# Latent attention of a two-layer encoder, written out as a fixed order of blocks on one Trainium2 core

## The chip, the cores and the metric

The kernel runs on one core of one Trainium2 chip. The metric is the device time of one execution in microseconds (us). Five engines work side by side, each through its own list of instructions: TensorE (PE in the profile, its weight loads PEld), VectorE (DVE), ScalarE (ACT), GpSimd (POOL) and SyncE (SP), which here only issues DMAs.

## The reference, cut to what matters

A trunk of two layers over 512 tokens of width 1024. Layer 0 is neighbourhood attention and a dense SwiGLU, layer 1 latent attention and a top-2-of-8 expert SwiGLU. The latent attention is what the change touches:

```python
c_q = _rmsnorm(down[..., :256]) * q_norm
c_kv = _rmsnorm(down[..., 256:384]) * kv_norm
q = (c_q @ w_uq).reshape(B, S, 16, 64 + 32)
kv = (c_kv @ w_ukv).reshape(B, S, 16, 64 + 64)
k_nope, v = kv[..., :64], kv[..., 64:]
...
s = (q_nope . k_nope + q_rope . k_rope) * scale      # 16 heads, 512 x 512
p = softmax(s, axis=-1)
o = p @ v                                            # then o @ w_o
```

Each of the two layers also has six vectors of 1024 values, `c_act @ w_ada[i] + b_ada[i]`, which shift, scale and gate its two halves.

## The kernel before, in words

All products that need full precision are made of three TensorE passes over a rounded part ("hi", `...H`) and a rest ("lo", `...L`). A split is therefore a cast of a tensor on ACT and a subtraction on DVE or POOL. `split_piece` is one such pair; `passes` (lines 295 to 297) issues the three matmuls.

The weights come through a list of jobs (`plan`). A job loads a raw tile (three slots), splits it (three slots) and is emitted when `need` first asks for it or looks ahead to it. Jobs of the kind "ada" add w_ada rows, weighted by c_act, into an accumulator on DVE (lines 223 and 225, eight per vector). The list strews the vectors (0, 2) to (1, 4) between the jobs of the first layer; vector (1, 5) stands behind the latent attention's weights (`add_ada(1, 5)`), and so falls in that stage.

`mla_phase` does the latent attention. Its loop goes over 8 pairs of heads; in a pair first the one head, then the other, each in four blocks of 128 queries against all 512 keys. A block is: three score matmuls of 512 columns; the row minimum of the (negated) scores on DVE (line 951); the exponential with its row sum on ACT (line 954); reciprocal and multiplication on DVE (955, 956); four transposes on TensorE (959); a copy out of PSUM on ACT (960). After a head's blocks `project(h + 2)` makes the queries of a later head (six matmuls; multiplication with the rotary table on DVE, cast on ACT, subtraction on POOL) and for every second head the keys of a pair (three matmuls, two splits). After both heads the products with the values follow (line 966): eight of 512 columns, then a split into `oH`, `oL`. Weights that fall due (`uq` 1, `mla_o`) are split by `need`, every second piece of 1024 columns on POOL (`MLA_POOL`).

None of this has an order of its own: a scheduler chooses before the run which instruction follows which on each engine, and it also places matmuls of the next stage (`mm<-oH`, `mm<-oL`: the output projection, three at a time in `mm` tiles of PSUM) into the attention. Two other parts of the kernel, the start (line 566) and the experts (line 1413), stand under `tc.manual_schedule()`: there each engine runs the block's instructions in the order in which the code issues them. Instructions from outside the block can still be placed between them.

PSUM is full: three `mm` tiles, two for scores, two for transposes, one for the sums `po`.

Of the kernel before, what the change touches and what calls it, by code (L numbers as in the profile page):

```python
# [19 lines left out]
P = 128  # L20
S = 512
D = 1024
KD = D // P
NH = 16
HD = 64
# [20 lines left out]
NKT = 3  # L46
MLA_POOL = 2
NQB = 4
# [10 lines left out]
class Kernel:  # L59
# [35 lines left out]

    def add_ada(self, layer, which):
        for j in range(4):
            self.jobs.append(("ada", (layer, which, j)))
# [336 lines left out]
    def plan(self):  # L435

        d = self.d
# [11 lines left out]
        bg = [(0, 2), (0, 3), (0, 4), (0, 5)] + [(1, w) for w in range(5)]  # L449
        bg = [(l, w, j) for l, w in bg for j in range(4)]  # L450
# [32 lines left out]
        self.add_ada(1, 5)  # L483
# [343 lines left out]
    def mla_phase(self, xT, hH, hL, norm):  # L827
        nc, tc, d = self.nc, self.tc, self.d
        scale = 96.0 ** -0.5
        with ExitStack() as es:  # L830
            pool = lambda name, bufs, **kw: es.enter_context(tc.tile_pool(name=name, bufs=bufs, **kw))
            st = self.mlap = pool("mla_static", 1)
            w2 = pool("mla_w2", 2)
            w3 = pool("mla_w3", 3)
# [13 lines left out]
            sq = w2.tile([P, 4, S], F32, name="pT")  # L848
            sq = [sq[:, i] for i in range(2)]
# [60 lines left out]
            qk = {}  # L910

            def project(h):
                hi, lo = self.need(("uq", h // 8), 0 if h < 2 else 1 if h < 8 else 2)
                ps = self.proj(hi, lo, h % 8, [cq[0][:, k] for k in range(2)], [cq[1][:, k] for k in range(2)], 2)
                q = [queries[:, h % NQB * 2 + z] for z in range(2)]
                t = self.stat2.tile([P, S], F32, name="t", tag="tmp")
                nc.vector.tensor_mul(t, ps, rope)
                nc.scalar.copy(q[0], t)
                (nc.gpsimd if h > 1 else nc.vector).tensor_tensor(q[1], t, q[0].bitcast(F32), op=OP.subtract)
                qk[h] = (q, kt[h % NKT])  # L920
                if h % 2:
                    return
                ps = self.mm.tile([P, S], F32, name="mm", tag="mm")
                wh, wl = (w[:, h:h + 2].rearrange("p h c -> p (h c)") for w in self.wk)
                self.passes(ps, wh, wl, ckv[0][:, 0], ckv[1][:, 0], True, True)
# [4 lines left out]
            queries = self.new_big("queries", F32R)  # L930
            oH, oL = self.new_big("oH", F32R), self.new_big("oL", F32R)
            self.pool_every = MLA_POOL
            with tc.high_priority():
                project(0)
                for k in kt[1:]:
                    for z in range(2):
                        nc.scalar.copy(k[z][64:128], kt[0][z][64:128].bitcast(F32))
                project(1)
            for pair in range(NH // 2):
                po = ps_o.tile([P, S], F32, name="po")  # L940
                PT = []
                for hh in range(2):
                    h = 2 * pair + hh
                    q, k = qk.pop(h)
                    pT = w2.tile([P, 4, S], F32, name="pT")
                    PT.append(pT)
                    for b in range(4):
                        s = ps_s.tile([P, S], F32, name="s")
                        self.passes(s, *(z[:, b * P:(b + 1) * P] for z in q), *k, True, True)
                        nm = w3.tile([P, 1], F32, name="nm")  # L950
                        nc.vector.tensor_reduce(nm, s, axis=AX.X, op=OP.min)
                        e = w3.tile([P, S], F32, name="e")
                        den = w3.tile([P, 1], F32, name="den")
                        nc.scalar.activation(e, s, AF.Exp, bias=nm, scale=-1.0, accum_out=den)
                        nc.vector.reciprocal(den, den)
                        nc.vector.tensor_scalar_mul(e, e, den)
                        pt = ps_t.tile([P, 4, P], F32, name="pt")
                        for t in range(4):
                            nc.tensor.transpose(pt[:, t], e[:, t * P:(t + 1) * P], self.ident)
                        nc.scalar.copy(pT[:, :, b * P:(b + 1) * P], pt)  # L960
                    if h + 2 < NH:
                        project(h + 2)
                for t in range(4):
                    for hh in range(2):
                        h = 2 * pair + hh
                        nc.tensor.matmul(po[hh * 64:hh * 64 + 64], V[:, t, h * HD:(h + 1) * HD], PT[hh][:, t],
                                         start=t == 0, stop=t == 3)
                self.split_piece(oH[:, pair], oL[:, pair], po)
            self.pool_every = 0
# [761 lines left out]
```

## Time and profile before

| | us |
|---|---|
| median of 3 runs | 1646.46 (1645.37 to 1647.16) |
| profiled execution | 1649.19 |
| its span, first to last instruction | 1647.3 |

The profile comes from that one profiled execution. Its times count from the first instruction of the span. A busy engine in a stretch is the sum of its instructions' times, and a matmul's time overlaps the next one's; so the distance between two starts is what a matmul takes of TensorE, not its duration. "[0.55 <-ACT hH]" behind an instruction means that its engine stood idle for 0.55 us before it, and that ACT's work on hH ended the wait.

### The profile page before, as it was taken

To read this page: it belongs to the slowest core of one execution; us is meant where nothing else is said; L and a number is where in the kernel's file an instruction comes from. 1 tells how busy PE (TensorE), PEld (TensorE's weight loads), DVE (VectorE), ACT (ScalarE), POOL (GpSimd) and SP (SyncE) were. 2 spreads that over 40 slices of the span, in tenths; PEclk is the share of its full clock that TensorE was granted. 3 is DMA by queue.
4 is the path that set the end of the run, shared out by engine and by line. 5 is a ranking of instruction groups with operands and counts; after the bars stand their busy time and mean duration, and the time that the engine had idled before them with its cause. 6 is when DMAs were issued, how large, how long until landed. Compare 5 with 4: busy or idle time off the path is not lost. (4 is left out here: it accounts for less than half of the span.)

```text
span 1647.3 us, 23092 instructions
## 1 busy us (share of the span) xinstructions
PE 1572.5 (95%) x7909; PEld 1245.2 (76%) x7909; DVE 1107.1 (67%) x1688; ACT 819.9 (50%) x1384; POOL 310.9 (19%) x259
## 2 busy tenths in 40 slices
PE   6899999999999999989999989999999999999996
PEld 4677779888888888856668677778887777777885
DVE  4687855765655434698865668656447888887765
ACT  3455544422222123577663656545436677765442
POOL 0332310002000000021101343112123324233310
PEclk9999999999999999999999989999999999999998
DMA  9545533467544523222112599758568999997751
GB/s 355 186 141 166 169 119 103 146 216 253 194 160 158 193 77 112 74 77 77 52 65 69 182 360 355 256 187 259 175 192 295 334 351 357 345 371 260 262 192 53
DMA packets 241209, 327.38 MB, mean 199 GB/s; under 512 B 9586, under 2 KB 191570, under 8 KB 240404
## 3 DMA queue, kind: packets, MB, share of 16 engines
q1 hardware_dynamic: 231072, 296.19, 54.0%
q0 software_dynamic: 5232, 18.09, 3.0%
q10 hardware_dynamic: 4740, 11.02, 1.8%
q8 instruction: 89, 1.46, 0.4%
q14 instruction: 76, 0.62, 0.1%
HBM read 308.75 MB, written 16.52 MB: 197 GB/s over the span
## 5 line engine op out<-in xcount | busy, mean ns | idle before, releaser
L198 DVE TENSOR_TENSOR lo<-raw,hi 128x1024 fp32r<-128x1024 f32 (+1 forms) x284 | 374.9, 1350 | 92.4 <-ACT hi L195 84.8
L195 ACT CAST hi<-raw 128x1024 fp32r<-128x1024 f32 (+1 forms) x319 | 318.3, 1045 | 225.0 <-PE mm L296 146.3
L296 PE MATMUL mm<-hL,hi 128*128 128x512 f32 x480 | 190.7, 397 | 0.0
L295 PE MATMUL mm<-hH,hi 128*128 128x512 f32 x480 | 190.1, 396 | 0.1
L297 PE MATMUL mm<-hH,lo 128*128 128x512 f32 x480 | 190.1, 396 | 0.0
L1245 PE MATMUL gu<-hi,he 128*128 128x512 f32 x360 | 144.5, 401 | 9.6 <-ACT act L1255 3.9
L198 POOL TENSOR_TENSOR lo<-raw,hi 128x1024 fp32r<-128x1024 f32 x39 | 101.6, 2606 | 236.1 <-ACT hi L195 187.0
L1247 PE MATMUL gu<-hi,he 128*128 128x512 f32 x360 | 141.2, 392 | 0.0
L1246 PE MATMUL gu<-lo,he 128*128 128x512 f32 x360 | 140.8, 391 | 0.0
L225 DVE SCALAR_TENSOR_TENSOR ada_acc<-raw,c_act,ada_acc 128x1024 f32<-128x1024 f32 x70 | 90.4, 1291 | 31.9 <-DMA raw<-in_w_ada_dram 31.3
L295 PEld LDWEIGHTS mm<-hH,hi 128*128 128x128 f32 x480 | 90.4, 188 | 20.9 <-ACT hi L195 0.5
L296 PEld LDWEIGHTS mm<-hL,hi 128*128 128x128 f32 x480 | 90.3, 188 | 19.9 <-issue 1.0
L297 PEld LDWEIGHTS mm<-hH,lo 128*128 128x128 f32 x480 | 90.4, 188 | 19.2 <-issue 0.2
L1245 PEld LDWEIGHTS gu<-hi,he 128*128 128x128 f32 x360 | 67.6, 188 | 30.6 <-issue 7.8
L1255 ACT ACTIVATE act<-gu 128x256 f32<-128x256 f32 x56 | 21.5, 384 | 138.8 <-PE gu L1247 138.8
L198 DVE TENSOR_TENSOR lo<-raws,hi 128x1024 fp32r<-128x1024 f32 x50 | 73.4, 1501 | 14.6 <-ACT hi L195 12.9
L1245 PE MATMUL y<-hi,a 128*128 128x512 f32 (+1 forms) x200 | 77.5, 387 | 2.2 <-PEq L1384 1.7
L1247 PEld LDWEIGHTS gu<-hi,he 128*128 128x128 f32 x360 | 67.6, 188 | 15.5 <-DVE he L209 0.4
L326 POOL TENSOR_TENSOR rs<-rs 128x2 f32<-128x2 f32 (+1 forms) x8 | 2.7, 336 | 402.4 <-DVE rs L324 402.4
L1246 PEld LDWEIGHTS gu<-lo,he 128*128 128x128 f32 x360 | 67.6, 188 | 13.2
L1247 PE MATMUL y<-hi,a 128*128 128x512 f32 (+1 forms) x200 | 75.4, 377 | 0.0
L1246 PE MATMUL y<-lo,a 128*128 128x512 f32 (+1 forms) x200 | 75.3, 376 | 0.0
(399 smaller groups left out, 3642.4 us busy)
## 6 DMA issues: line engine op xcount, KB each, us to landing
raw<-in_moe_w_gu_dram SPq DMA_DIRECT2D x176, 512.0 KB
raw<-in_w_ada_dram SPq DMA_DIRECT2D x48, 1024.0 KB
raw<-in_moe_w_down_dram SPq DMA_DIRECT2D x37, 1024.0 KB
raws<-in_moe_w_gu_dram SPq DMA_DIRECT2D x48, 512.0 KB
raw<-in_ffn_w_gu_dram SPq DMA_DIRECT2D x22, 1024.0 KB
raw<-in_na_w_qkv_dram SPq DMA_DIRECT2D x12, 1024.0 KB
raws<-in_moe_w_down_dram SPq DMA_DIRECT2D x11, 1024.0 KB
raw<-in_ffn_w_down_dram SPq DMA_DIRECT2D x8, 1024.0 KB
```

The source lines that it names most:

```text
L195: nc.scalar.copy(hi[:, c], raw[:, c])
L198: eng.tensor_tensor(lo[:, c], raw[:, c], hi[:, c].bitcast(F32), op=OP.subtract)
L225: nc.vector.scalar_tensor_tensor(acc, raw[:, i], c, acc, op0=OP.mult, op1=OP.add)
L295: nc.tensor.matmul(ps, ah, bh, start=first, stop=False)
L296: nc.tensor.matmul(ps, ah, bl, start=False, stop=False)
L297: nc.tensor.matmul(ps, al, bh, start=False, stop=last)
L326: g.tensor_tensor(w, y, y, op=OP.mult)
L1245: nc.tensor.matmul(ps, xh, wh, start=first, stop=False)
L1246: nc.tensor.matmul(ps, xh, wl, start=False, stop=False)
L1247: nc.tensor.matmul(ps, xl, wh, start=False, stop=last)
L1255: nc.scalar.activation(a, ps[:, 0:256], AF.Silu)
```

## The change

The vectors (1, 5) go into the strewn list, four jobs more there and four fewer in the latent attention. `kt` has four buffers instead of three. The tiles `pT` hold one block (four buffers of 512 columns a partition) instead of one head. The loop of `mla_phase` becomes a loop over the 64 blocks, in which blocks of the two heads of a pair alternate, under `tc.manual_schedule()`. In step `u` are issued, in this order: the scores of block u + 2, the transposes of u, the division of u + 1, the copy of u, the minimum and the exponential of u + 2, in even steps the products with the values of two blocks, in three of four odd steps five or six matmuls of a projection, then up to two owed splits, then pieces of weight splits. All subtractions but every second one of `mla_o` are on DVE. Three of the four `mla_o` jobs are split in the loop.

```diff
-NKT = 3
-MLA_POOL = 2
+NKT = 4
...
-        bg = [(0, 2), (0, 3), (0, 4), (0, 5)] + [(1, w) for w in range(5)]
+        bg = [(0, 2), (0, 3), (0, 4), (0, 5)] + [(1, w) for w in range(6)]
...
-        self.add_ada(1, 5)
...
-            w2 = pool("mla_w2", 2)
+            w4 = pool("mla_w4", 4)
...
+            def queries_of(h):
+                hi, lo = self.done[("uq", h // 8)][0:2]
...
+                for n, (w, x, k) in enumerate(ops):
+                    nc.tensor.matmul(ps, w[:, k, c], x[k], start=n == 0, stop=n == 5)
+                    yield
+                q = pair_q(h)
+                t = self.stat2.tile([P, S], F32, name="t", tag="tmp")
+                owed.append(lambda: (nc.vector.tensor_mul(t, ps, rope), nc.scalar.copy(q[0], t)))
+                owed.append(lambda: nc.vector.tensor_sub(q[1], t, q[0].bitcast(F32)))
+
+            def keys_of(pair):
...
+                for n, (w, x) in enumerate(ops):
+                    nc.tensor.matmul(ps, w, x[:, 0], start=n == 0, stop=n == 2)
+                    yield
                 for i in range(2):
                     kh, kl = kt[(h + i) % NKT]
-                    self.split_piece(kh[0:64], kl[0:64], ps[i * 64:i * 64 + 64])
+                    owed.append(lambda i=i, kh=kh, kl=kl: self.split_piece(kh[0:64], kl[0:64], ps[i * 64:i * 64 + 64]))
+
+            def project(pair):
+                yield from queries_of(2 * pair)
+                yield from keys_of(pair)
+                yield from queries_of(2 * pair + 1)
+
+            def weights(ahead):
...
+                for n, (x, y, r) in enumerate(pairs):
+                    nc.scalar.copy(x, r)
+                    yield
+                    (nc.gpsimd if n % 2 and perm is None else nc.vector).tensor_tensor(y, r, x.bitcast(F32), op=OP.subtract)
+                    yield
...
+            def head(u):
+                return u // 8 * 2 + u % 2, u // 2 % 4
...
+            def values_of(d):
+                pair, b = divmod(d, 4)
...
+                for t in range(4):
+                    for i in range(2):
+                        h = 2 * pair + i
+                        nc.tensor.matmul(po[i * 64:i * 64 + 64, b * P:(b + 1) * P], V[:, t, h * HD:(h + 1) * HD], PT[2 * d + i][:, t],
                                          start=t == 0, stop=t == 3)
...
+                if b == 3:
+                    owed.append(lambda: self.split_piece(oH[:, pair], oL[:, pair], po))
+
+            spread = {4: 2, 6: 2, 8: 2, 10: 2, 12: 2, 14: 2, 22: 1, 24: 1, 26: 1, 28: 1, 30: 1, 32: 1, 34: 1, 36: 1, 56: 1, 58: 1, 60: 1, 62: 1}
+            work = (x for ahead in (3, 2, 1, 0) for x in weights(ahead))
+            chunks = {}
+            with tc.manual_schedule():
+                for u in range(-2, 8 * NH // 2):
+                    if u + 2 < 8 * NH // 2:
+                        scores(u + 2)
+                    if u >= 0:
+                        pt = turn(u)
+                    if 0 <= u + 1 < 8 * NH // 2:
+                        shares(u + 1)
+                    if u >= 0:
+                        PT[u] = w4.tile([P, 4, P], F32, name="pT")
+                        nc.scalar.copy(PT[u], pt)
+                    if u + 2 < 8 * NH // 2:
+                        largest(u + 2)
+                        exponentials(u + 2)
+                    todo, owed = owed[0:2], owed[2:]
+                    if u % 2 == 0 and u > 0:
+                        values_of(u // 2 - 1)
+                    if u % 2:
+                        i = (u - 1) // 2
+                        pair, c = divmod(i + 5, 4)
+                        if c < 3 and pair < NH // 2:
+                            if c == 0:
+                                chunks = project(pair)
+                            for _ in range(5):
+                                next(chunks, None)
+                            if c == 2:
+                                next(chunks, None)
+                    for f in todo:
+                        f()
+                    for _ in range(spread.get(u, 0)):
+                        next(work, None)
+                values_of(4 * NH // 2 - 1)
+                while owed:
+                    owed.pop(0)()
+                for _ in work:
+                    pass
```

`scores`, `turn`, `largest`, `exponentials` and `shares` hold the same instructions as lines 949 to 960, one block each: `shares` is the reciprocal and the multiplication, `turn` the four transposes.

## Rows read from the trace of the kernel before

**Rows 1.** Stretches of the span: each engine's busy us (instructions), granted clock, DMA share, GB/s.
```profile
711.00:864.00 153.00, 146.89 (x703) 93.45 (x704) 126.30 (x250) 108.36 (x237) 21.97 (x16) 1.00 0.19 64
560.00:660.00 100.00, 99.94 (x491) 83.52 (x490) 38.74 (x53) 28.83 (x42) 0.00 (x0) 1.00 0.27 89
```
**Rows 2.** The timeline where the attention begins: start us, us, engine, line, out<-in.
```profile
709.99 2.17 DVE L209 TENSOR_TENSOR ktL<-t,ktH 64x512 fp32r<-64x512 f32 x1
...
716.60 0.69 ACT L954 ACTIVATE e<-s,nm 128x512 f32<-128x512 f32 x1
```
**Rows 3.** The timeline where the attention's last sums are taken over.
```profile
871.25 0.59 ACT L208 CAST oH<-po 128x512 fp32r<-128x512 f32 x1 [5.77 <-PE po L966]
```
**Rows 4.** Groups by line and shape, 711 to 872 us: count | busy us, mean ns | idle before.
```profile
L918 ACT CAST queries<-t 128x512 fp32r<-128x512 f32 x15 | 9.4, 624 | 0.5 <-DVE den L955 0.3 <-DVE t L917 0.2
L208 ACT CAST ktH<-mm 64x512 fp32r<-64x512 f32 x15 | 8.7, 581 | 1.0 <-PE s L297 0.8
...
L296 PE MATMUL mm<-oL,hi 128*128 128x512 f32 x20 | 8.3, 415 | 0.0
...
L919 DVE TENSOR_TENSOR queries<-t,queries 128x512 fp32r<-128x512 f32 x2 | 1.4, 677 | 0.0
```
**Rows 5.** The timeline of DVE at the end of the attention.
```profile
856.11 0.49 DVE L956 TENSOR_SCALAR e<-e,den 128x512 f32<-128x512 f32 x1
856.51 0.69 DVE L951 TENSOR_REDUCE nm<-s 128x1 f32<-128x512 f32 x1
857.11 0.16 DVE L955 RECIPROCAL den<-den 128x1 f32<-128x1 f32 x1
...
858.04 0.17 DVE L955 RECIPROCAL den<-den 128x1 f32<-128x1 f32 x1 [0.25 <-ACT e L954]
858.25 0.49 DVE L956 TENSOR_SCALAR e<-e,den 128x512 f32<-128x512 f32 x1
```
**Rows 6.** The timeline of ACT in the same stretch.
```profile
855.25 0.19 ACT L954 ACTIVATION_READ_ACCUMULATOR e<-s,nm 128x1 f32 x1
855.35 0.57 ACT L960 COPY pT<-pt 128x512 f32<-128x512 f32 x1
...
857.23 0.69 ACT L954 ACTIVATE e<-s,nm 128x512 f32<-128x512 f32 x1 [0.41 <-DVE nm L951]
857.82 0.19 ACT L954 ACTIVATION_READ_ACCUMULATOR e<-s,nm 128x1 f32 x1
```
**Rows 7.** The timeline of DVE in the hand-ordered start.
```profile
24.14 1.41 DVE L372 SCALAR_TENSOR_TENSOR hL<-mod_t,mod,hH 128x512 fp32r<-128x512 f32 x2 [0.55 <-ACT hH L366]
25.48 2.35 DVE L198 TENSOR_TENSOR lo<-raw,hi 128x1024 fp32r<-128x1024 f32 x2
```
**Rows 8.** The timeline of TensorE around one block's transposes.
```profile
752.10 0.40 PE L295 MATMUL mm<-cqH,hi 128*128 128x512 f32 x1
752.33 0.60 PE L959 MATMUL pt<-ident,e 128*128 128x128 f32 x4
752.68 0.48 PE L296 MATMUL mm<-cqL,hi 128*128 128x512 f32 x1
```
**Rows 9.** The timeline of TensorE in layer 0's attention, with products of one block.
```profile
152.46 0.66 PE L709 MATMUL po<-pT,V 128*64 128x128 f32 x8
```
**Rows 10.** Groups by line and shape, 690 to 722 us.
```profile
L209 DVE TENSOR_TENSOR lo<-raw,hi 128x768 fp32r<-128x768 f32 x4 | 3.8, 954 | 2.2 <-ACT hi L208 2.2
L208 ACT CAST hi<-raw 128x768 fp32r<-128x768 f32 x4 | 3.3, 837 | 0.0
L208 ACT CAST hi<-raw 128x128 fp32r<-128x128 f32 x8 | 2.2, 310 | 0.0
```
**Rows 11.** The timeline of POOL and DVE while a weight piece is split.
```profile
756.07 2.55 POOL L198 TENSOR_TENSOR lo<-raw,hi 128x1024 fp32r<-128x1024 f32 x1
...
756.65 2.25 DVE L956 TENSOR_SCALAR e<-e,den 128x512 f32<-128x512 f32 x1
```
**Rows 12.** A stretch of the span just before the attention, columns as in rows 1.
```profile
695.20:699.00 3.80, 3.80 (x15) 3.17 (x16) 2.05 (x8) 2.40 (x7) 0.30 (x1) 0.59 0.00 0
```

More of the change, by code (lines that the diff above doesn't have):

```diff
@@ L94, in add_split @@
         self.jobs.append(("split", key, srcs, nk, cols, perm))
-    def add_ada(self, layer, which):
-        for j in range(4):
-            self.jobs.append(("ada", (layer, which, j)))
     def need(self, key, ahead=1):
@@ L847, in mla_phase @@
             V = st.tile([P, 4, D], F32, name="V")
-            sq = w2.tile([P, 4, S], F32, name="pT")
-            sq = [sq[:, i] for i in range(2)]
+            sq = [w4.tile([P, 4, P], F32, name="pT").rearrange("p a b -> p (a b)") for _ in range(2)]
             def latent(psums, tok):
@@ L909, in mla_phase @@
                 values(t)
[L910 to L915, printed above, removed]
-                t = self.stat2.tile([P, S], F32, name="t", tag="tmp")
[L917 to L922, printed above, removed]
+            queries = self.new_big("queries", F32R)
@@ L969, in mla_phase @@
-            self.pool_every = 0
+                    owed.append(lambda i=i, kh=kh, kl=kl: self.split_piece(kh[0:64], kl[0:64], ps[i * 64:i * 64 + 64]))
[4 more added lines that the diff above has]
+            def weights(ahead):
+                job = self.jobs[self.emitted]
+                raw = self.loaded.pop(self.emitted)
+                _, key, _, nk, cols, perm = job
+                hi, lo = self.split_tiles([P, nk, cols])
+                self.done[key] = (hi, lo, self.emitted)
+                self.emitted += 1
+                self.preload(ahead)
+                pairs = []
+                if perm is not None:
+                    for k in range(2):
+                        r, x, y = (z[:, k].rearrange("p (h c) -> p h c", h=8) for z in (raw, hi, lo))
+                        pairs.append((x[:, :, 0:96], y[:, :, 0:96], r))
+                        two = "p a (i two) -> p a i two"
+                        x, y, r = (z.rearrange(two, two=2) for z in (x[:, :, 96:128], y[:, :, 96:128], r[:, :, 64:96]))
+                        pairs += [(x[:, :, :, i], y[:, :, :, i], r[:, :, :, 1 - i]) for i in range(2)]
+                else:
+                    pairs = [(hi[:, a:a + 4], lo[:, a:a + 4], raw[:, a:a + 4]) for a in (0, 4)]
+                for n, (x, y, r) in enumerate(pairs):
[3 more added lines that the diff above has]
+                    yield
@@ new lines, in mla_phase @@
+            owed = []
+            E, NM, DEN, SC, PT = {}, {}, {}, {}, {}
+            self.need(("uq", 0), 0)
+            self.preload(3)
+            with tc.high_priority():
+                for _ in project(0):
+                    while owed:
+                        owed.pop(0)()
+                while owed:
+                    owed.pop(0)()
+                for n, k in enumerate(kt[1:]):
+                    for z in range(2):
+                        (nc.scalar.copy if n == 0 else nc.gpsimd.tensor_copy)(k[z][64:128], kt[0][z][64:128].bitcast(F32))
```

70 lines of the change are left out of this document (34 added, 36 removed).

## The prediction

> **What bounds the kernel now.** The busy times by stretch come first: in the attention TensorE is busy for 146.9 of 153.0 us, DVE for 126.3, ACT for 108.4 [rows 1]. The reader is to see that TensorE is nearly full there at its full clock, and that no other engine is far behind. Part of that filling is not the attention's own: the groups by line show 20 matmuls of the output projection in one of its three passes (20 and 19 in the others), so 59 in all, placed between the blocks [rows 4]. At 0.23 us from start to start [rows 8] they are 13.6 us of later work done early. The timeline gives the edges: the first exponential at 716.6, the last sums taken over at 871.25 [rows 2, 3]. This is the stretch to redo under the new order; before and after it TensorE's work is the same.
>
> Then the timelines of DVE and ACT say how long one block's chain is, and the timeline of the start says what a hand-written order means: there DVE waits 0.55 us for ACT's hH, while the weight subtractions issued behind it run only afterwards, without any wait of their own [rows 7]. An instruction that waits holds up all that was issued after it on its engine. So I cost the new loop by who stands behind whom.
>
> **The loop of one step.** On DVE the order is division of block u+1, minimum of u+2, owed splits, division of u+2, minimum of u+3. The division of u+2 needs its exponential, and the exponential of u+3 needs a minimum that stands behind that division. That is a closed ring with no way past it. Count from the start of an exponential, E: its sum is read from E+0.59 (857.23 to 857.82) for 0.19 [rows 6]; the reciprocal starts 0.03 later, at E+0.81 (858.01 to 858.04), the multiplication 0.21 after it, the next minimum 0.40 after that (856.11 to 856.51), and lasts 0.69 [rows 5]; the next exponential starts 0.03 later (857.20 to 857.23) [rows 5, 6]. Sum: 0.59 + 0.19 + 0.03 + 0.21 + 0.40 + 0.69 + 0.03 = 2.14 us a block, 17.1 for the eight blocks of a pair.
>
> **TensorE's side of it.** A pair has 24 score matmuls at 0.23 = 5.5; 8 groups of transposes at 0.35 (752.33 to 752.68), up to 0.45 with the slower matmul behind them, 2.8 to 3.6 [rows 8]; 15 projection matmuls, 3.5; and the products with the values, now of 128 columns. The attention of layer 0 has such products, half as many in a block, at 0.66 [rows 9]; four times 1.32 = 5.3. Sum 17.1 to 17.9. TensorE alone would thus fill the ring's time, and may run ahead of it by the second score buffer. The smaller matmuls cost no more than this; the four-fold number matters only if the ring is not the longer one.
>
> **The owed splits lengthen the ring.** They stand on DVE between a minimum and the next division. Each begins with a cast that ACT takes up only after the exponential: 0.10 after the reading of its sum starts (855.25 to 855.35), so at E+0.69 [rows 6].
> - Queries: cast 0.62, so done at E+1.31; subtraction from E+1.34; the next instruction follows 0.60 after the start of one that long (856.51 to 857.11) [rows 4, 5]. The reciprocal starts at E+1.94 instead of E+0.81: +1.13. Twice a pair.
> - Keys: two casts of 0.58, two subtractions, from E+1.30 and E+1.90: reciprocal at E+2.50, +1.69 [rows 4, 5].
> - Sums oH: cast 0.59 [rows 3], reciprocal at E+1.91: +1.10.
>
> They fall into different steps (u = 2, 3, 4 and 9 of a pair's eight), so they add: 1.13 + 1.69 + 1.13 + 1.10 = 5.05 us a pair. Seven pairs are projected inside the loop and seven sums are split in it: 35.4. A pair then takes 17.1 + 5.05 = 22.2 us.
>
> **Weight pieces.** uq 1: twice a 768-column cast and subtraction behind a query split, each about +1.1 (0.84 + 0.95, less what overlaps), and four small pieces at 0.25 to 0.45 [rows 10]: 3.8. mla_o: three DVE pieces whose cast is long done, about 0.27 over the time in which DVE would have waited: 0.8. Three POOL pieces: while one ran for 2.55 us, a multiplication took 2.25 instead of 0.49 [rows 5, 11]. So each costs between nothing (it meets a minimum, which reads PSUM) and 1.76; I take half, 2.6 in all, and keep 0 to 5.3 for the range. [...]
>
> **Start, end and what was done early.** Before, the first exponential waited behind a key split that took 2.17 us, against 0.68 for a subtraction of queries of the same width, and behind one 768-column subtraction of uq 1 (0.95) [rows 2, 4, 10]. Both reasons move into the loop; the first exponential comes at 716.6 - 1.5 - 0.95 = 714.15. Copies of the rotary keys on POOL are due a pair later: nothing. The last of 64 exponentials starts 63 x 2.14 = 134.8, plus 35.4 + 3.8 + 0.8 + 2.6 later: 714.15 + 177.4 = 891.6. Behind it come division (done at E+1.51), transposes, copy (0.57 [rows 6]) and products (1.3): the sums are taken over at about E+4.2, 895.8, against 871.25 [rows 3]: +24.5 us. After the last projection (u = 51) TensorE has some 9 us of gaps, room for about 39 of the 59 early matmuls; 20 are lost, 4.6 us. If none fits it is 13.6, if all fit 0. Sum: +29.1.
>
> **Vector (1, 5).** Its eight DVE additions leave the attention, where DVE now waits anyway, and go into the dense layer, where DVE is busy for 38.7 of 100 us and TensorE for 99.9 [rows 1]. TensorE covers them; without that cover they would be some 10 us, two passes over each of four raw tiles. SP issues their four loads between the dense layer's instead of the attention's, through the same three raw slots, at a DMA share of 0.27 [rows 1]; what waits behind them on SP is the next weights' load, one job ahead of its use. I take 0.
>
> **Sum.** 1649.19 + 29.1 = 1678.3 for the profiled execution. It lies 2.7 above the median of the runs shown, so 1675.6, say **1676 us**. Its own range is 1663 (POOL pieces free, all early matmuls fit, splits overlap a fifth better) to 1691 (the opposite).
>
> **Rivals.**
> - *TensorE sets the pace, faster than before.* If the owed casts did not wait behind the exponential, a pair would take TensorE's 17.1 to 17.9 us. The loop then lasts 133 to 140 us (the last pair projects nothing), ends near 852 and, with 4 us behind it and 13.6 of lost early work, stands between 6 us earlier and level: -3, **1643**. This decides from about 18 us a pair downwards. For it: TensorE's 17.9 us are near the ring's 17.1. Against it: DVE takes things in turn in the one hand-ordered part that I read [rows 7]. 14%.
> - *TensorE's clock falls as well.* With 17.9 of 22.2 us of work, TensorE has gaps of 1 to 1.7 us in four steps of eight. Just before the attention, after a gap of that size and a few tiny matmuls, the granted clock was 0.59 for 3.8 us [rows 12]; in the attention, at 147 of 153, it was 1.00 [rows 1]. One such stretch a pair would cost at most 3.8 x 0.41 = 1.6 us, two would be 25 in all; taken as 16, **1692**. [...]
> - *The order is not what runs.* If instructions were still rearranged, the attention would stay near its present time: **1646**. Against it speaks [rows 7] again. 6%.
>
> **Chances.** Forecast 73%, the three rivals 14, 7 and 6%. What a measurement of this kernel tells from no change is about 0.2%, 3.3 us. Faster takes over half of the first rival and a third of the last: 10%. Within 0.2%: the rest of these two but a little, 8%. Slower: 82%. The range 1640 to 1698 takes in the forecast's own, the clock, and half of the first rival.
>
> **What would show it.** Right: in steps without owed splits the starts of exponentials lie 2.1 to 2.2 us apart, in steps with query or key splits 3.3 and 3.8; DVE's waits name ACT casts of queries, ktH and oH; TensorE is busy for some 80% of the loop, with gaps; the sums are taken over at about 896. Wrong: exponentials 2.3 us apart throughout with TensorE full (first rival), a granted clock under 0.95 in the loop (second), or DVE doing a division ahead of a split that was issued before it (third). Most likely to be off is the cost of the splits: if casts of owed splits start before the exponential, 35 us go.

## The result, and the profile after

| | before | after |
|---|---|---|
| median, same chip (us) | 1646.81 (1645.37 to 1648.81, 6 runs) | 1682.16 (1679.54 to 1683.85, 6 runs) |
| profiled execution, its span | 1649.19, 1647.3 | 1682.73, 1680.9 |
| first and last of 64 exponentials | 716.60, 860.14 | 712.10, 899.46 |
| last cast of the sums oH | 871.25 | 907.04 |
| from there to the end of the span | 776.05 | 773.9 |

The kernel became slower by a ratio of 1.0218 [1.0207, 1.023], 35.4 us between the medians. All of it lies between the start of the attention and the last sums: they are taken over 35.8 us later than in [rows 3], and what follows is 2.2 us shorter.

First the stretches of the changed kernel, with the columns of [rows 1] (us, busy time of the engines, granted clock, DMA):

```profile
560.00:640.00 80.00, 79.94 (x347) 64.90 (x346) 38.16 (x45) 21.16 (x30) 0.00 (x0) 1.00 0.40 130
720.00:760.00 40.00, 30.79 (x210) 22.71 (x209) 26.03 (x56) 23.04 (x53) 0.00 (x0) 0.88 0.00 1
760.00:800.00 40.00, 36.30 (x235) 28.17 (x234) 24.80 (x53) 22.57 (x51) 0.91 (x1) 0.86 0.08 27
800.00:840.00 40.00, 33.92 (x221) 25.20 (x219) 24.43 (x51) 23.40 (x51) 4.08 (x2) 0.83 0.17 54
```

TensorE, busy for 146.9 of 153.0 us in [rows 1], now has gaps, and its granted clock has fallen below 1.00. No other engine is busier for it: DVE is down to 60 to 65% here. Time goes into waits, so the timelines come next. ACT, from plain steps into a step with a query split and one with the key split:

```profile
717.29 0.69 ACT L993 ACTIVATE e<-s,nm 128x512 f32<-128x512 f32 x1
...
719.43 0.69 ACT L993 ACTIVATE e<-s,nm 128x512 f32<-128x512 f32 x1 [0.88 <-DVE nm L988]
...
721.56 0.69 ACT L993 ACTIVATE e<-s,nm 128x512 f32<-128x512 f32 x1 [0.74 <-DVE nm L988]
...
722.24 0.61 ACT L919 CAST queries<-t 128x512 fp32r<-128x512 f32 x1
...
724.80 0.69 ACT L993 ACTIVATE e<-s,nm 128x512 f32<-128x512 f32 x1 [1.47 <-DVE nm L988]
...
725.48 0.56 ACT L203 CAST ktH<-mm 64x512 fp32r<-64x512 f32 x1
726.80 0.58 ACT L203 CAST ktH<-mm 64x512 fp32r<-64x512 f32 x1 [0.75 <-DVE ktL L204]
...
729.45 0.69 ACT L993 ACTIVATE e<-s,nm 128x512 f32<-128x512 f32 x1 [1.46 <-DVE nm L988]
```

The exponentials are 2.14 and 2.13 us apart in plain steps, 3.24 with the query split, 4.65 with the key split. All but the first of them wait for a minimum (nm). DVE in the same stretch:

```profile
722.88 0.69 DVE L920 TENSOR_TENSOR queries<-t,queries 128x512 fp32r<-128x512 f32 x1 [0.76 <-ACT queries L919]
...
726.08 0.68 DVE L204 TENSOR_TENSOR ktL<-mm,ktH 64x512 fp32r<-64x512 f32 x1 [1.31 <-ACT ktH L203]
727.41 0.69 DVE L204 TENSOR_TENSOR ktL<-mm,ktH 64x512 fp32r<-64x512 f32 x1 [0.65 <-ACT ktH L203]
728.03 0.15 DVE L996 RECIPROCAL den<-den 128x1 f32<-128x1 f32 x1
```

The division of the next block (728.03) has nothing to wait for by then; it stands behind subtractions that wait for ACT. In the last row ahead of it DVE waits once more, because the second cast in turn waited 0.75 us for the first subtraction. The waits from 713 to 900 us, in us in total, times and longest, say how much this is:

```profile
ACT e L993 <- DVE nm L988: 46.0, 40, 1.7
DVE den L996 <- ACT e L993: 28.2, 29, 1.6
...
DVE ktL L204 <- ACT ktH L203: 13.7, 14, 1.3
DVE queries L920 <- ACT queries L919: 10.6, 14, 0.8
DVE oL L204 <- ACT oH L203: 10.3, 7, 1.6
...
ACT ktH L203 <- DVE ktL L204: 5.2, 7, 0.8
```

The three DVE waits for a split's cast sum to 34.6 us. That is close to what was lost, but a sum of waits is no proof of a cause: the experiments have to show that the time goes when these waits go.

The second thing to see is TensorE once a pair, after the key step. Stretches of 2 us, then three rows of its timeline:

```profile
776.00:778.00 2.00, 1.93 (x20) 1.28 (x19) 0.68 (x1) 1.25 (x4) 0.00 (x0) 1.00 0.00 0
778.00:780.00 2.00, 0.33 (x3) 0.36 (x4) 1.70 (x4) 0.79 (x2) 0.00 (x0) 1.00 0.00 0
780.00:782.00 2.00, 1.19 (x5) 0.85 (x4) 1.24 (x3) 1.72 (x4) 0.00 (x0) 0.80 0.00 0
782.00:784.00 2.00, 1.69 (x6) 0.72 (x4) 1.45 (x4) 0.53 (x2) 0.00 (x0) 0.50 0.00 0
784.00:786.00 2.00, 2.00 (x18) 1.62 (x17) 1.25 (x3) 1.15 (x4) 0.00 (x0) 0.50 0.00 0
```

```profile
779.67 0.63 PE L1003 MATMUL pt<-ident,e 128*128 128x128 f32 x4 [1.74 <-DVE e L997]
781.11 0.76 PE L290 MATMUL s<-ktH,queries 128*128 128x512 f32 x1 [0.81 <-ACT e L993]
...
784.05 1.98 PE L1015 MATMUL po<-pT,V 128*64 128x128 f32 x16
```

TensorE stands idle for 1.74 us behind the key split and for 0.81 us soon after; then the granted clock is 0.50 for some 7 us; it falls so behind six of the seven key splits. Sixteen products with the values take 1.98 us there, against 1.09 at a granted clock of 1.00. The intervals between exponentials in the steps behind it (u mod 8 = 6, 7 and 0) have means of 2.79, 2.38 and 2.32 us instead of 2.13.

### The profile page after: what moved, and what is told of

Same layout as the page of the kernel before. It is cut to its first block, busy times and chain, and to the rows that moved or that the text cites. A ratio compares the mean times of both kernels' runs of the same rounds, so it can differ in the third digit from the quotient of the medians.

```text
span 1680.9 us, 23885 instructions
## 1 busy us (share of the span) xinstructions
PE 1591.3 (95%) x8293; PEld 1278.8 (76%) x8293; DVE 1108.4 (66%) x1701; ACT 818.9 (49%) x1382; POOL 297.0 (18%) x250
## 5 line engine op out<-in xcount | busy, mean ns | idle before, releaser
L190 ACT CAST hi<-raw 128x1024 fp32r<-128x1024 f32 (+1 forms) x313 | 312.0, 1045 | 223.5 <-PE mm L291 145.3
L193 POOL TENSOR_TENSOR lo<-raw,hi 128x1024 fp32r<-128x1024 f32 x37 | 97.1, 2624 | 226.7 <-ACT hi L190 162.5
L193 DVE TENSOR_TENSOR lo<-raws,hi 128x1024 fp32r<-128x1024 f32 x50 | 68.4, 1401 | 14.3 <-ACT hi L190 11.7
L290 PE MATMUL mm<-aH,hi 128*128 128x512 f32 (+1 forms) x200 | 74.0, 370 | 0.0
```

Of the source, the lines that this page charges most:

```text
L190: nc.scalar.copy(hi[:, c], raw[:, c])
L193: eng.tensor_tensor(lo[:, c], raw[:, c], hi[:, c].bitcast(F32), op=OP.subtract)
L290: nc.tensor.matmul(ps, ah, bh, start=first, stop=False)
```

## The experiments

Twelve kernels were run in three batches, each beside the kernel before on the same chip (1644.97, 1644.74 and 1645.64 us). "Loop" is the time from the first to the last exponential; 187.36 in the changed kernel, 143.54 before.

| run | us (lowest to highest) | ratio to before | loop |
|---|---|---|---|
| changed kernel | 1682.16 (1679.54 to 1683.85) | 1.0218 [1.0207, 1.023] | 187.36 |
| 1 subtractions a step later | 1661.55 (1660.9 to 1667.66) | 1.010 [1.0085, 1.0116] | 165.47 |
| 2 minimum ahead of the division | 1683.33 (1680.88 to 1686.22) | 1.024 [1.0224, 1.0255] | 179.11 |
| 3 both | 1666.59 (1664.75 to 1668.72) | 1.0132 [1.0116, 1.0147] | 163.92 |
| 4 both key casts first | 1679.10 (1678.11 to 1680.61) | 1.0208 [1.0194, 1.0222] | 185.13 |
| 5 casts ahead of the exponential | 1654.58 (1651.46 to 1656.48) | 1.0056 [1.0042, 1.007] | 154.24 |
| 6 scores three times, once a pair | 1683.32 (1680.27 to 1684.17) | 1.0227 [1.0213, 1.0241] | 183.09 |
| 7 before, products by block | 1646.83 (1643.64 to 1651.2) | 1.0011 [1.0002, 1.002] | |
| 8 before, vector (1, 5) moved | 1648.17 (1645.68 to 1651.05) | 1.002 [1.001, 1.0029] | 146.34 |
| 9 as 5, vector moved back | 1658.13 (1656.75 to 1659.97) | 1.0072 [1.0056, 1.0088] | 160.38 |
| 10 as 9, low parts earlier | 1656.15 (1654.46 to 1657.33) | 1.0059 [1.0043, 1.0074] | 157.83 |
| 11 as 10, minimum first | 1660.95 (1658.92 to 1663.0) | 1.0091 [1.0075, 1.0108] | 156.29 |
| 12 changed, keys in two tiles | 1674.82 (1671.13 to 1675.51) | 1.0163 [1.0144, 1.0182] | 176.24 |

The theory was the prediction's: the owed splits make DVE wait for casts of the same step, and this lengthens a closed ring between DVE and ACT. The rivals were the ring itself without the splits, TensorE's clock, and the smaller products or the moved vector.

**1. Subtractions one step later.** Casts are issued as before; each subtraction is kept for the next step, when its cast is long done.

```diff
...
-                    todo, owed = owed[0:2], owed[2:]
+                    for f in late:
+                        f()
+                    todo, owed, late = owed[0:1], owed[1:], []
...
-                    for f in todo:
-                        f()
+                    for f, g in todo:
+                        f()
+                        late.append(g)
```

> The changed kernel with one thing undone: an owed split's subtraction is issued one step after its cast, so that its cast is done when VectorE comes to it. Ring theory (the closed chain exponential, division, minimum, exponential of 2.13 us a block, lengthened by owed splits that wait on VectorE for casts standing behind the exponential): the waits of 5.8 us a pair shrink to some 1.2 (three operations in one step), 32 us less; the stretches at a lower TensorE clock, which follow the longest of these waits, go too, up to 9 us less; fewer gaps for the output projection's early matmuls, 0 to 8 us more: 1641 to 1655 us, exponentials 2.13 us apart in most steps. Clock theory (TensorE at half clock once a pair is itself what costs): no more than 9 us less, 1673 or above. Small-products theory (the products with the values of 128 columns cost the time): no change beyond 5 us, 1677 or above.

Some 20 us went by the medians, fewer than expected. The trace is of the slowest of the four executions, 1667.66 us. The postponed subtraction of the sums oH made a wait of its own: the next pair's products need the sums' buffer, and TensorE stood for it. Its row in the waits of this kernel (us in total, times, longest):

```profile
PE po L1017 <- DVE oL L1023: 10.6, 6, 2.1
```

Also, 42 matmuls of the output projection were done ahead of the last sums, 63 in the changed kernel: at 0.23 us [rows 8] 4.8 us are left for later.

**2. The minimum ahead of the division.** This opens the ring and leaves the owed splits alone.

```diff
+                    if u + 2 < 8 * NH // 2:
+                        largest(u + 2)
                     if 0 <= u + 1 < 8 * NH // 2:
                         shares(u + 1)
...
-                        largest(u + 2)
                         exponentials(u + 2)
```

> The changed kernel with two instructions exchanged on VectorE: the minimum of block u+2 is issued before the division of block u+1. Ring theory: the ring is open; steps without owed splits may come down to TensorE's 2.2 us or less, those with query splits to about 2.7, with key splits to about 3.9, and TensorE can catch up between: a pair takes 18 to 19.5 us instead of 24, 36 to 48 us less, and 0 to 10 of it is given back by early matmuls that find no gaps: 1636 to 1656 us. Clock theory: the waits behind casts remain, and so does the dip of the clock: 1673 or above. Small-products theory: no change beyond 5 us.

No gain. The loop is 8.3 us shorter, but the last sums come at 904.75 against 907.04: the exponentials run ahead of TensorE's work, and the time is handed back behind the last of them. The waits of this kernel show a new releaser of the minimum, a longer wait of TensorE's transposes for the division (23.2 us, 15.0 in the changed kernel), and the splits' waits still there:

```profile
DVE nm L988 <- PE s L292: 29.9, 23, 2.8
...
PE pt L1003 <- DVE e L997: 23.2, 14, 2.8
...
DVE queries L920 <- ACT queries L919: 9.6, 14, 0.7
DVE ktL L204 <- ACT ktH L203: 8.1, 12, 0.7
```

So the ring of exponential, division and minimum, though measured at the forecast 2.13 us, is not what the end hangs on by itself: other waits stand just behind it. They are not TensorE's own work, since TensorE is busy for only 30.6 to 33.8 us of each 40 from 720 to 840. By the order of issue the edit closes another ring, from a minimum over the division that now stands behind it, TensorE's transposes and the scores issued after them to a later minimum; this is argued, and no run opens that ring.

**3. Both edits of runs 1 and 2.**

> The changed kernel with both edits: subtractions a step later, minimum before division. Ring theory: no chain is left that is longer than TensorE's own work, 17.1 to 17.9 us a pair; the loop ends 8 x (24.0 - 17.7) = 50 us earlier, some 11 us of early output projection lost with the gaps: 1638 to 1648 us, TensorE over 95% busy in the loop at full clock. Clock theory and small-products theory: 1670 or above; by the small products TensorE would be full at well over 18 us a pair.

A miss: no better than run 1, by the medians 5 us worse. Plain steps do reach 1.62 us in one place (u mod 8 = 5), but TensorE, busy for 32.3 to 33.6 us of each 40, still waits: from 715 to 860 us 9.8 us for the low part of the sums and 12.7 for divisions. What sets the mean over a pair here is not shown.

**4. Both key casts ahead of both subtractions.**

```diff
-                    owed.append(lambda i=i, kh=kh, kl=kl: self.split_piece(kh[0:64], kl[0:64], ps[i * 64:i * 64 + 64]))
+                ks = [(*kt[(h + i) % NKT], ps[i * 64:i * 64 + 64]) for i in range(2)]
+                owed.append(lambda: [nc.scalar.copy(kh[0:64], p) for kh, kl, p in ks])
+                owed.append(lambda: [nc.vector.tensor_sub(kl[0:64], p, kh[0:64].bitcast(F32)) for kh, kl, p in ks])
```

> The changed kernel with the two key splits of a pair issued as cast, cast, subtraction, subtraction instead of cast, subtraction, cast, subtraction. The second cast now starts 0.75 us after the first cast's end, behind the first subtraction. Ring theory: step with key splits 4.65 to about 3.85 us, 7 x 0.8 = 5.6 us less; if the shorter wait also spares TensorE the lower clock, up to 9 us more: 1667 to 1677 us. If the second cast waits for something else than the subtraction (for ScalarE itself, or PSUM): no change, 1682.

Only 3 us by the medians and the intervals of the ratios overlap; the key step is still 4.61 us. Two rows of the timeline, each of two instructions in a row, say why:

```profile
773.20 1.16 ACT L931 CAST ktH<-mm 64x512 fp32r<-64x512 f32 x2
...
774.39 1.39 DVE L932 TENSOR_TENSOR ktL<-mm,ktH 64x512 fp32r<-64x512 f32 x2 [1.91 <-ACT ktH L931]
```

The casts now follow each other, but the first subtraction, whose own cast was done near 773.8, starts at 774.39, when the second one is done. The two halves of the keys are read from one PSUM tile (mm). In both orders the later reader of that tile, on the other engine, started only when the reader issued ahead of it had ended: here at 774.39 after an end at 774.36, in the changed kernel at 726.80 after 726.76.

The key step itself thus gained 0.3 us over seven pairs. But this run prices the clock. In the second, fourth and sixth pair the granted clock stays at 0.50 for some 7 us behind the key step, and the interval at u mod 8 = 6 is 3.38 us; in the third and fifth it stays there half as long, and the interval is 2.13. (In the first pair the clock is back soon after this step begins.) Two stretches of this kernel, each from 4 us after the clock's fall, in the third pair and in the fourth:

```profile
782.00:784.00 2.00, 2.00 (x16) 1.56 (x13) 1.12 (x4) 1.50 (x3) 0.00 (x0) 1.00 0.00 0
...
806.00:808.00 2.00, 2.00 (x8) 1.60 (x8) 1.14 (x3) 1.24 (x3) 0.00 (x0) 0.50 0.01 4
```

So within one kernel and one order, the longer stretch costs 1.25 us in that step and 0.4 to 0.5 in the next, and the shorter one nothing.

**12. Keys in two tiles.** The keys' three matmuls are made twice, into a PSUM tile for each head, in the changed kernel.

```diff
-                ps = self.mm.tile([P, S], F32, name="mm", tag="mm")
+                ps = [self.mm.tile([P, S], F32, name="mm", tag="mm") for _ in range(2)]
...
-                for n, (w, x) in enumerate(ops):
-                    nc.tensor.matmul(ps, w, x[:, 0], start=n == 0, stop=n == 2)
-                    yield
+                for z in ps:
+                    for n, (w, x) in enumerate(ops):
+                        nc.tensor.matmul(z, w, x[:, 0], start=n == 0, stop=n == 2)
+                        yield
...
-                            for _ in range(5):
+                            for _ in range((5, 7, 6)[c]):
```

> The changed kernel with the keys of the two heads of a pair in a PSUM tile each (three more matmuls a pair, and the key split falls one step later). If the second cast is late because both engines take turns on one PSUM tile, the second cast follows the first at once and the key step falls from 4.6 to the forecast 3.83 us: seven times 0.8 is 5.5 us, so 1675 to 1678. If the order of issue or the engines themselves are the cause, the key step stays and the time with it: 1681 to 1685.

7.3 us less by the medians (the ratios 1.0163 and 1.0218 stand 9 us apart). Timeline, then two stretches of this kernel:

```profile
774.59 1.17 ACT L203 CAST ktH<-mm 64x512 fp32r<-64x512 f32 x2
...
775.19 1.41 DVE L204 TENSOR_TENSOR ktL<-mm,ktH 64x512 fp32r<-64x512 f32 x2 [1.31 <-ACT ktH L203]
```

```profile
720.00:760.00 40.00, 32.86 (x234) 23.78 (x231) 26.74 (x59) 24.16 (x55) 0.00 (x0) 1.00 0.00 1
760.00:800.00 40.00, 34.22 (x244) 25.35 (x242) 26.82 (x56) 24.43 (x54) 2.47 (x1) 1.00 0.16 53
```

With the cast-subtract order of the changed kernel, the second cast no longer waits, the first subtraction overlaps it, and the key step takes 4.03 us instead of 4.65: 4.3 us over seven pairs. So the shared tile was the cause of the second cast's wait. The trace also tells who asks for it. In the changed kernel the second cast carries a wait for the semaphore (a counter by which engines wait for each other, number 106 in the trace) that the first subtraction raises; in run 4 the first cast raises none, and the first subtraction waits for the one that the second cast raises; here the second cast carries no wait for DVE. It is an order that the program asks for. But the loop shrank by 11.1 us: here the granted clock stays at 1.00 but for some 3 us near 800, and the steps behind the key step take 2.23, 2.14 and 2.23 us instead of 2.79, 2.38 and 2.32, together 0.89 a pair. The run thus moved two things, and by this sum the clock's share is about 6 us. Which of the three, the shorter gap, the three matmuls more or the key split's later step, kept the clock up isn't told apart.

**6. Scores three times, once a pair.** In the gap behind the key split TensorE computes one block's scores three times over (each starts afresh, so the last counts).

```diff
                         scores(u + 2)
+                        if u > 0 and u % 8 == 4:
+                            again(u + 2)
```

> The changed kernel with extra work: once a pair, in the step in which TensorE stood idle behind the key splits, the scores' three matmuls are made three times over, 1.4 us more of TensorE in a gap of 1.7. The result is the same. Clock theory: TensorE falls to half clock because of this gap, 5 us a pair, and that costs 1.1 to 1.4 us a pair in the three steps behind it; kept busy, it stays at full clock and the time falls by 7 to 10 us: 1672 to 1675. Ring theory without the clock: the steps behind it are long for another reason; no change, or up to 3 us slower: 1682 to 1685.

The total did not move, which the ring theory expected, yet it does not refute the clock. In the three stretches from 720 to 840 the granted clock rose from between 0.83 and 0.88 to between 0.93 and 0.96, and the loop lost 4.3 us:

```profile
760.00:800.00 40.00, 36.04 (x249) 28.20 (x248) 25.01 (x55) 23.93 (x53) 1.16 (x1) 0.94 0.08 27
800.00:840.00 40.00, 34.35 (x243) 26.23 (x242) 25.47 (x54) 23.92 (x53) 3.87 (x2) 0.96 0.16 54
```

But the extra matmuls took the room of others: 48 matmuls of the output projection were done ahead of the last sums, 63 in the changed kernel. Fifteen at 0.23 us [rows 8] are 3.5 us to be done later. Filling a gap is paid for in the work that had already filled it.

**5. Casts ahead of the exponential.** Owed work is planned by step: a cast is issued ahead of the step's exponential, from operands of an earlier step, and a subtraction behind the minimum, at most two in a step. Matmuls and ring stay as they are.

```diff
...
+                    for f in plan.pop((u, 0), ()):
+                        f()
                     if u + 2 < 8 * NH // 2:
                         exponentials(u + 2)
+                    for f in plan.pop((u, 1), ()):
+                        f()
-                    todo, owed = owed[0:2], owed[2:]
...
+                put(t_at, 1, lambda: nc.vector.tensor_mul(t, ps, rope))
+                put(q_at, 0, lambda: nc.scalar.copy(q[0], t))
+                put(l_at, 1, lambda: nc.vector.tensor_sub(q[1], t, q[0].bitcast(F32)))
...
+                yield from queries_of(2 * pair, s(3), s(4), s(4))
+                yield from keys_of(pair, (s(3), s(5), s(5), s(6)))
+                yield from queries_of(2 * pair + 1, s(5), s(6), s(7))
```

> The changed kernel with each owed split taken apart and placed by hand: its cast stands on ScalarE ahead of a step's exponential, its subtraction on VectorE behind that step's minimum, one or two VectorE operations a step; everything else as in the changed kernel. In the first run of the late subtractions a third operation in one step and the products that waited for oL left 1.8 us of new waits in two steps of eight. Ring theory: now no owed split waits; ring 2.13 us a block against TensorE's 2.3 us, a pair takes 17.4 to 18.2 us instead of 24.0, the last exponential comes 45 to 50 us earlier, and the output projection's early matmuls (50 of them, 11 us) partly fall out: 1641 to 1655 us. If TensorE or the scheduler's placing of other work sets the pace above that, as in the run with the minimum first: 1660 or above.

1654.58: 27.6 us of the 35.4 are back by the placing of the splits alone, the multiplications with the rotary table among them. Stretches and waits of this kernel:

```profile
720.00:760.00 40.00, 35.70 (x266) 27.24 (x267) 31.31 (x68) 28.12 (x64) 0.00 (x0) 1.00 0.08 27
760.00:800.00 40.00, 36.89 (x277) 28.11 (x277) 32.86 (x67) 28.43 (x63) 2.39 (x1) 1.00 0.08 27
```

```profile
PE s L292 <- DVE queries L927: 6.3, 6, 1.0
...
DVE oL L1029 <- ACT oH L1028: 5.0, 7, 0.9
...
DVE queries L927 <- ACT queries L926: 2.7, 5, 0.7
...
DVE ktL L941 <- ACT ktH L940: 1.6, 4, 0.4
```

DVE's three waits for a split's cast sum to 9.3 us instead of 34.6; more than half of what is left is that for the sums oH. The gaps are smaller and the clock is whole, so these 27.6 us hold the clock's share as well. New is a wait of the scores for the second head's subtraction. Why this kernel stays 9.8 us behind the kernel before was not settled.

**7 and 8. The kernel before with one part of the change each.** Run 7 takes the products with the values per block of 128 columns, run 8 moves vector (1, 5) to the dense layer.

```diff
...
+                for b in range(4):
                     for t in range(4):
                         for hh in range(2):
                             h = 2 * pair + hh
-                            nc.tensor.matmul(po[hh * 64:hh * 64 + 64], V[:, t, h * HD:(h + 1) * HD], PT[hh][:, t],
+                            nc.tensor.matmul(po[hh * 64:hh * 64 + 64, b * P:(b + 1) * P], V[:, t, h * HD:(h + 1) * HD], PT[4 * hh + b][:, t],
```

```diff
-        bg = [(0, 2), (0, 3), (0, 4), (0, 5)] + [(1, w) for w in range(5)]
+        bg = [(0, 2), (0, 3), (0, 4), (0, 5)] + [(1, w) for w in range(6)]
...
-        self.add_ada(1, 5)
```

> The kernel before with one part of the change alone: products with the values of 128 columns, eight for each block of a pair, instead of eight of 512 columns; order still the scheduler's. Small-products theory: this part carries much of the loss, 15 us or more. Ring theory: TensorE's own time rises by 0.3 to 0.7 us a pair: 1645 to 1652, at most 6 us slower.

> The kernel before with one part of the change alone: the four jobs of vector (1, 5) stand in the first layer's list. Prediction: covered by TensorE in the dense layer, and no gain in the attention either, within 3 us of the kernel before. Rival: ten us of VectorE work leave a stage in which VectorE is 83% busy, and up to 10 us go with them; or the four loads delay the dense layer's weights and it is slower by as much.

The products cost about 2 us. The move cost 3.4, at the edge of what was expected. In run 8's trace little of it went into the dense layer: from the first row statistics ahead of the dense layer to the first of this attention it is 408.85 us, 407.77 before; the loop is 2.8 us longer, although DVE has eight additions less in it. Why the attention of the kernel before gets longer when they leave wasn't found.

**9, 10 and 11. Further from run 5.** Run 9 takes run 8's edit out of run 5, so that the vector's jobs stand behind the attention's weights again; run 10 also takes the low parts earlier (its edit below); run 11 also takes the minimum first, with the edit of run 2.

```diff
-                yield from keys_of(pair, (s(3), s(5), s(5), s(6)))
-                yield from queries_of(2 * pair + 1, s(5), s(6), s(7))
+                yield from keys_of(pair, (s(3), s(4), s(5), s(5)))
+                yield from queries_of(2 * pair + 1, s(5), s(6), s(6))
```

> Changed on the kernel that places the owed casts ahead of the exponential (1654.6 us): vector (1, 5) stays among the jobs behind the latent attention's weights, as in the kernel before, and is no longer formed in the dense layer. If the 3.4 us that the kernel before lost by this move alone are paid in the dense layer, this gains as much: 1650 to 1653. If they were paid in the attention, whose order is now written by hand, no change: 1653 to 1657. If the eight additions now meet the output projection, it loses: 1657 and more.

> Changed on the kernel with the vector back: the second queries of a pair get their low part in the step of its cast, one step earlier, and the low parts of both keys come one step earlier too. The scores then no longer wait for VectorE's subtraction, a wait of 6.3 us in six places. If this wait sets the end, 4 to 6 us less: 1645 to 1648, level with the kernel before. If TensorE's own work sets the end (18.2 of 20 us busy), 0 to 2 us less.

> Changed on the kernel with the low parts earlier: VectorE takes the minimum of block u+2 ahead of the division of block u+1, so that the ring of 2.14 us is opened. If the ring still holds the loop anywhere, 2 to 5 us less. If TensorE sets the pace, no change within 2 us; the exponentials then run further ahead and the stretch behind the last one gets longer by as much.

Run 9 went the way that none but its last alternative foresaw, and at another place: the additions did not meet the output projection but the loop, which got 6.1 us longer. They are not part of the hand order and slip in between. DVE in run 9:

```profile
809.25 0.75 DVE L222 TENSOR_SCALAR ada_acc<-raw,c_act 128x1024 f32<-128x1024 f32 x1 [0.24 <-DMA raw<-in_w_ada_dram]
809.91 0.15 DVE L1009 RECIPROCAL den<-den 128x1 f32<-128x1 f32 x1
810.03 1.28 DVE L224 SCALAR_TENSOR_TENSOR ada_acc<-raw,c_act,ada_acc 128x1024 f32<-128x1024 f32 x1
811.24 0.48 DVE L1010 TENSOR_SCALAR e<-e,den 128x512 f32<-128x512 f32 x1
```

An addition of 1.28 us stands between the two halves of a division, on the ring. Under this order, then, moving the vector away was worth 3.5 us by the medians (runs 5 and 9) and 2.6 by the ratios, whose intervals overlap, the opposite of what run 8 showed. Run 10's scores have no wait for DVE's queries left among the larger ones, and it is 2 us below run 9 instead of the 4 to 6 expected of a wait that sets the end; the intervals overlap. Run 11 is 4.8 us above run 10: putting the minimum first loses here. No version beat the kernel before; the nearest is run 5, by 1.0056 [1.0042, 1.007]. Run 5 with run 10's edit was not run.

## Why the prediction was right, point by point

The sum for the profiled execution was +29.1; it measured +33.5, and the mechanism is the one predicted: a closed ring, lengthened by owed splits. That the two numbers lie so close is in part luck. The first exponential came 2.05 us earlier than forecast and the loop was 10.0 longer; the tail was 3.4 longer, and the stretch behind it, with no early work lost, 6.8 shorter. Some 6 us of the loop are the clock's, a rival's mechanism, and a granted clock under 0.95 was among the signs that the prediction gave against itself. The stated ends of the range, 1663 and 1691, do not come out of their own terms either: 2.6 or 2.7 for the POOL pieces, a fifth of 35.4 and 4.6 (below) or 9.0 (above) for the early matmuls give about 1661 and 1694. By its terms:

- **The ring.** Forecast 2.14 us a block, measured 2.13 in the plain step (u mod 8 = 5, seven pairs). That TensorE may stand close behind was said too. The opened ring gave nothing (runs 2 and 3), but TensorE was not full there; other waits took the ring's place.
- **The owed splits.** Queries: forecast +1.13, measured +1.11 (3.24). Sums oH: +1.10, measured +1.08 (3.21). Keys: +1.69, measured **+2.52** (4.65). This is the mis-sized term: the prediction let ACT make both casts in a row, and none of its rows shows two casts from one PSUM tile. In the trace the second cast waits for the first subtraction (0.75 of ACT's time), and run 12, with a tile for each head, brings 4.03, still 0.2 above the forecast's 3.83. 0.83 over seven pairs is 5.8 us. That the waits are the cause and not only beside it: run 5 moves nothing but the splits, and 27.6 us go.
- **The clock.** Held for a rival with 7%, it did fall, to between 0.83 and 0.91 in stretches of 40 us, but not at the price given there (16 to 25 us). Run 12 and the steps behind the key step put it at 0.89 us a pair, some 6 us; run 4, where it can be read within one kernel, at about 1.7 us behind a long stretch and nothing behind a short one. In the changed kernel's trace it is 0.50 behind six of seven key splits, in the pair shown above behind gaps of 1.74 and 0.81 us.
- **Weight pieces.** Forecast 7.2 for all. By intervals that stand out in run 12, where the clock doesn't blur them, uq 1 costs 1.0 and 0.9 in two steps, and the others 0.2 to 0.4 in some eight: between 4 and 5 us. The POOL pieces, taken at 2.6, cost nothing that is seen in the changed kernel: of the two in the loop, one ran from 799.09 to 801.56, while DVE made a minimum of the usual 0.69 and then waited for a key cast. The third, from 899.13, did stretch the last multiplication to 1.33 us instead of 0.49, while TensorE was full. In run 12 the steps in which the two in the loop run take 2.53 us each, against 2.13 or 2.14 in the same step of the other five pairs, and in run 9 one met a subtraction, which took 1.99 instead of 0.69. So a piece cost nothing where it met a minimum, 0.84 us where it met the last multiplication, and 1.30 us where it met run 9's subtraction; the prediction's half of 1.76 for each was an estimate between such cases.
- **The loop in sum.** 187.36 against a forecast of 177.4: +5.8 by the keys, some +6 by the clock, some -3 by the weights, 9 of the 10 us.
- **Start.** Forecast 2.45 us earlier. From the attention's first statistics to the first exponential it is 30.58 us, 31.98 before: 1.4 gained. The 2.17 us of [rows 2] were one subtraction that ran while POOL split a piece (709.02 to 711.61); in the changed kernel the same subtraction takes 0.69. The other 3.1 of the 4.5 in the table were there before: the row statistics ahead of the dense layer, up to which the change touches nothing, already start 3.5 us earlier in this execution.
- **Tail.** Forecast 4.2 us from the last exponential to the sums, measured 7.6. The last two copies wait 2.01 and 1.76 us for TensorE's transposes and the cast of oH 1.86 us for its products: TensorE is behind at the end, which the forecast's chain without queueing left out; it is busy without a gap from 895 to 907, with 16 early matmuls of the output projection behind the last exponential.
- **Early matmuls.** Forecast: 20 of 59 lost, 4.6 us. Measured: 63 (three times 21) ahead of the last cast of oH, none lost. By the same count it was 56 before, and 31 of these stood behind the last exponential and not between the blocks. Seven more at 0.23 are 1.6 of the 2.2 us by which the end became shorter. This error and the one before have opposite signs.
- **Vector (1, 5).** Taken as 0. In the dense layer DVE is busy for 38.2 of 80 us instead of 27.35, TensorE for 79.94 as before, and from the row statistics ahead of the dense layer to those of the attention it is 408.14 us against 407.77. Right in this kernel; run 8's 3.4 us belong to the other order.

Of the rivals, "TensorE sets the pace" is what run 5 comes near to, at 1654.6 and not at 1643, with TensorE busy for 35.7 to 36.9 us of 40; it took what the prediction named as most likely to be off, casts that start before the exponential. "The order is not what runs" is refuted by the rows of DVE above for what the hand order holds, while run 9 shows that other work still slips between.

## What to carry to other kernels

In an order written by hand, put a cast and the subtraction that needs it in different steps, the cast ahead of the step's long instruction and the subtraction behind work that is ready anyway: here this alone was worth 27.6 us, the clock's share included. Count the pieces of one PSUM tile that two engines read as a chain in the order of issue, and give each its own tile where the chain stands on the loop's ring: here this took the key step from 4.65 to 4.03 us (run 12). Opening a ring pays only as far as the next wait is away (nothing here), and work put into TensorE's gaps has to be counted against the later work that was already done in them.

## What was not expected of the hardware

- Two halves of one PSUM tile, read by ACT and DVE, were read in the order of issue, in both orders tried: 0.75 us of ACT's time in one, a subtraction 0.6 us late in the other, neither with two tiles. The trace shows it as a wait for the other engine and not as a slower read: the casts last 0.56 to 0.58 us either way. The program asks for it, by the semaphores that its instructions carry (run 12); what the chip would do without them was not tried.
- A granted clock of 0.50 came behind two gaps, 1.74 and 0.81 us in the pair shown, with a little work between and around them, and lasted some 7 us; yet it cost only 0.89 us a pair, and where it lasted half as long (run 4) nothing. That most steps leave TensorE idle time, in which it can catch up, would explain it, but this is argued and not measured.
